# Keeping two kinds of operand sums of the output stage on chip for both pairs, and loading the first residual rows later

## The chip, the cores and the metric

The kernel runs on one core of a Trainium2 chip. The metric is the device time of one execution in microseconds (us); lower is better. The kernel before took 1652.37 us, the median of 3 runs (1649.89 to 1652.61).

## The reference

Two layers over 512 tokens of width 2048. What matters here is the end of each layer: one output projection with a 2048 x 2048 weight, a norm over the 2048 columns, and the residual. All arithmetic is float32.

```python
def hybrid_layer(x, w_in, w_out, g_pre, g_post, ...):
    h = rmsnorm(x, g_pre)
    z = h @ w_in
    ...   # gated linear attention gives o_gla, chunked attention gives o_att
    y = jnp.concatenate([o_gla, o_att], axis=-1) @ w_out
    return x + rmsnorm(y, g_post)

def reference(x, w_in, w_out, g_pre, g_post, ...):
    h = x
    for l in range(DEPTH):
        h = hybrid_layer(h, w_in[l], w_out[l], g_pre[l], g_post[l], ...)
    return h
```

## The kernel before, in words

**Products.** Weights come in blocks of 512 columns. Two blocks make a pair, and a pair is multiplied in Strassen-Winograd form: seven products P1 to P7 instead of eight. Each runs over four chunks c of the contracted dimension. One product for one chunk is 12 matmuls of 128x128 by 128x512 (line 523): every float32 number is split into a high and a low part, and three of the four part products are kept. Below, "a product" means one name for one chunk, such as P6 of chunk 2.

**What a product needs.** On the weight side each job passes four steps: `load` (line 187, a 512 KB DMA on SP's queue), `bring` (line 218, a 512 KB load of the token operand from DRAM into one of the four tiles tagged `sa`, where that operand isn't on chip), `high` (line 238, for most kinds a sum or difference of two weight blocks on DVE at lines 246 or 249, and a copy to the high part on ACT at line 257) and `low` (line 260, the rest, on DVE at line 263, into one of three tiles). `ahead` (line 313) keeps these steps three to five products ahead of the matmuls. On the token side P1, P2 and P4 take plain blocks; P5 takes the sum S1, P6 takes S2, P3 takes S4 and P7 takes S3 (table `LEFT`, line 160).

**The output stage** is `paired_out` (line 1570). Its first pair is columns 0 to 1023 of the output weight (`n` = 0), its second pair the rest (`n` = 2). Chunks go in the order 2, 3, 0, 1 (`C_END`). The order of products is: P1 of the second pair, P1 of the first, P2 of the second, P2 of the first. Then the first pair's P5 (four chunks), the middle (P6 2, P3 2, P6 3, P3 3, P6 0, P6 1, P3 0, P3 1), P7 and P4, and then the same for the second pair: 56 products.

**The sums** of this stage are made by `paired_sums` (line 1432), chunk after chunk, four for each: S1, S2, S4, S3. Each is one DVE addition over 128x512 (line 1447) and a split into high and low parts (a cast on ACT at line 113, a subtraction on DVE at line 114). The result goes into a tile and from there to DRAM through GpSimd's queue (line 1456). S1 has a tile for each chunk (`g6`, `g7`, `g14`, `g15`), and the first pair reads it there; S2, S4 and S3 take turns in two tiles, `g2` and `g3`. `bring` (line 236) loads them back: S2, S4 and S3 for each pair, S1 for the second. A sum's inputs come from DRAM by `load_parts` (line 1423). For chunks 2 and 3 they lie in `sa` tiles (two each), for chunk 0 in `a110` and `a111`, for chunk 1 in two `sa` tiles again. The fourth input is on chip as `og_full`, in a tile of the ring `t2`, which has eight.

**Order.** Side work (attention heads, sums, the finish of tokens) is written as generators, and `pump` (line 323) advances them: `rate` steps after each product. `tc.issue_after` puts one instruction behind another on its engine. The tile framework then orders each engine's instructions by a simulated timeline, with program order as priority, and places the waits. The sums of chunks 0 and 1 begin once the first result of the second pair's P2 is taken (`"first" in issued`). `project` (line 1519) takes a result tile: a square on ACT and a multiplication with the norm's gain on DVE (line 1529). The gains of the stage are loaded by `load_gains` (line 1585) into `a112` and `a113`, and in layer 0 twice more by `load_gain` (line 1513).

**Residual rows.** `load_tokens` (line 620, DMAs at line 616) loads the rows that are added to the result: half 0 into `g6`, `g7`, `g12`, `g13`, half 1 into `g9`, `g10` and four smaller tiles. Before, both halves are issued on GpSimd's queue after the first pair's P7 and P4 of chunk 2, when all sums have been written out. `finish` (line 1556) uses them from the second pair's P7 (layer 0) or P4 (layer 1) on, and in layer 0 goes on with `prep_half` (line 762), which makes the next layer's operands in the tiles `a11..` and `a12..`.

Of the kernel before, what the change touches and what calls it, by code (L numbers as in the profile page):

```python
# [9 lines left out]
F32R = mybir.dt.float32r  # L10
BF16 = mybir.dt.bfloat16
AF = mybir.ActivationFunctionType
ALU = mybir.AluOpType
# [3 lines left out]
P = 128  # L17
# [3 lines left out]
W = 512  # L21
# [14 lines left out]
def hybrid_trunk(  # L36
# [141 lines left out]
    class Job:  # L178
# [39 lines left out]
        def bring(self):  # L218
# [6 lines left out]
            if end and name == "S1" and not p.get("second"):  # L225
                return
# [193 lines left out]
    class Pair:  # L420
# [60 lines left out]
        def operand(self, job, k, c):  # L481
            if job.a is not None:
                return job.a
            if self.end and k == "P5":
                until(lambda: ("S1", c) in A)
                return A["S1", c]
# [400 lines left out]
    def layer(l):  # L887
# [544 lines left out]
        def paired_sums():  # L1432
            spare = 0
            for i, c in enumerate(C_END):
                while c not in og_full or c not in parts and i < 3 or i > 1 and "first" not in issued:
                    yield
                if c not in parts:
                    load_parts(c, [rtile("sa", (2, 512), F32R) for _ in range(2)])
                    yield
                a11, a21, a12, _ = parts[c]  # L1440
                a22 = og_full[c]
                for name, out, in0, in1, op in (
                    ("S1", a22, a21, a22, ALU.subtract), ("S2", a22, a22, a11, ALU.subtract),
                    ("S4", a12, a12, a22, ALU.add), ("S3", a21, a11, a21, ALU.subtract),
                ):
                    with tc.issue_after(last_out[0] or last_state[0]):
                        nc.vector.tensor_tensor(out=out, in0=in0, in1=in1, op=op)
# [5 lines left out]
                    z = slot(tag, [2, 512], F32R)  # L1453
                    with tc.issue_after(last_cast[0]):
                        split(z[:, 0, :], z[:, 1, :], out)
# [43 lines left out]
        values.run(early_rest(C_IN)[-4:], rate=6 if paired else 4, after=fetch_operands)  # L1499
# [252 lines left out]
```

## Time and profile before

| what | value |
|---|---|
| median of the runs | 1652.37 us |
| the profiled execution's own time | 1650.46 us |
| its span on the core | 1648.7 us |
| TensorE (PE) busy | 97% of the span |
| VectorE (DVE) busy | 78% |
| ScalarE (ACT) busy | 57% |
| GpSimd (POOL) busy | 10% |
| mean granted TensorE clock | 0.988 of full speed |
| HBM read, written | 403.50 MB, 65.82 MB |

How to read it: the page gives each engine's busy time; a busy PE is not a PE at its peak, because matmuls are pipelined, so the pace is best taken from start to start of matmuls, or from a stretch's length over its number of products. The waits view says which instruction waited for what, with the total, the count and the longest wait. The windows view gives for a stretch its length, each engine's busy time (and instructions), the granted clock, the busy share of the DMA engines and the GB/s moved. The timeline lists start, length and the idle time before an instruction, with what ended it.

### The profile page before, as it was taken

The numbers are of one execution on the slowest core, as the hardware profiler recorded it, in microseconds if no ns is written. First come the engines' busy times: TensorE is split into PE (matmuls) and PEld (weight loads), VectorE is DVE, ScalarE is ACT, GpSimd is POOL, SyncE is SP. The second block draws the span as 40 slices with busy tenths as digits, with TensorE's granted clock in tenths as the row PEclk, the third lists the DMA queues.
The fourth block names the chain that finished last, engine by engine and source line by source line (L and its number), as shares of the span: only waits on it lengthen the run. The fifth ranks groups of instructions, "written<-read, shape, count | busy, mean of one in ns | idle before, by whom it ended". The sixth has DMA issues, their size and how long they took to land.

```text
span 1648.7 us, 24344 instructions
## 1 busy us (share of the span) xinstructions
PE 1597.6 (97%) x8722; PEld 1344.8 (82%) x8722; DVE 1293.2 (78%) x1600; ACT 946.7 (57%) x1562; POOL 172.9 (10%) x290
## 2 busy tenths in 40 slices
PE   9999999999999999979999999999999999998797
PEld 6787889999988876657877888899999887766575
DVE  6788976877876776958879888868688767869588
ACT  8565544555676545635596555446567765556253
POOL 1131000000001001120132100000010000011101
PEclk9999999999999999989999999999999999999898
DMA  9999966858776696989969898768596857968996
GB/s 373 342 342 351 320 232 233 302 193 295 255 244 222 219 345 242 331 311 387 342 230 349 302 337 320 262 222 289 180 310 213 280 172 273 370 226 301 350 355 229
DMA packets 150553, 472.02 MB, mean 286 GB/s; under 512 B 16428, under 2 KB 35892, under 8 KB 150432
## 3 DMA queue, kind: packets, MB, share of 16 engines
q1 hardware_dynamic: 128384, 394.18, 68.0%
q0 software_dynamic: 21472, 75.33, 11.8%
q8 instruction: 69, 1.13, 0.3%
q10 hardware_dynamic: 576, 0.95, 0.2%
q14 instruction: 52, 0.43, 0.1%
HBM read 403.50 MB, written 65.82 MB: 285 GB/s over the span
## 4 chain that ended last, share of the span: by engine, by line
PE 75%; DMA 10%; DVE 6%; issue 6%; ACT 2%; POOL 1%; SPq 0%; POOLq 0%; ACTq 0%; DVEq 0%
PE mm L523 47%; PE mm L508 20%; DMA raw<-in_w_dram 5%; DVE wl L263 3%; PE ax L1122 2%; DMA H<-in_w_dram 2%; DMA sa<-oS 2%; DMA sa<-A 1%; DVE H L246 1%; PE ax L1328 1%; PE ax L1105 1%; ACT wh L257 1%; PE ax L1292 1%; PE ax L717 1%; PE ax L1085 1%
## 5 line engine op out<-in xcount | busy, mean ns | idle before, releaser
L523 PE MATMUL mm<-wh,sa 128*128 128x512 f32 x1280 | 419.2, 401 | 28.1 <-DMA sa<-oS 22.7
L257 ACT CAST wh<-H 128x1024 fp32r<-128x1024 f32 x263 | 275.9, 1051 | 238.1 <-PE mm L523 99.9
L263 DVE TENSOR_TENSOR wl<-H,wh 128x1024 fp32r<-128x1024 f32 (+1 forms) x265 | 321.7, 1217 | 100.3 <-PE mm L523 41.2
L263 DVE TENSOR_TENSOR wl<-raw,wh 128x1024 fp32r<-128x1024 f32 x240 | 292.8, 1221 | 100.0 <-PE mm L523 46.8
L257 ACT CAST wh<-raw 128x1024 fp32r<-128x1024 f32 x240 | 252.3, 1052 | 195.3 <-PE mm L523 107.2
L523 PEld LDWEIGHTS mm<-wh,sa 128*128 128x128 f32 x1280 | 243.8, 192 | 91.9 <-issue 20.8
L523 PE MATMUL mm<-wh,g 128*128 128x512 f32 x960 | 300.0, 391 | 0.0
L523 PE MATMUL mm<-wh,a 128*128 128x512 f32 x896 | 289.7, 396 | 2.9 <-ACT pc L446 1.6
L246 DVE TENSOR_TENSOR H<-H,raw 128x1024 f32<-128x1024 f32 x192 | 232.7, 1220 | 31.1 <-DMA raw<-in_w_dram 22.3
L523 PE MATMUL mm<-wl,sa 128*128 128x512 f32 x640 | 255.1, 399 | 0.2 <-DVE wl L263 0.2
L508 PE MATMUL mm<-sa,wh 128*128 128x256 f32 x1280 | 236.0, 285 | 0.0
L523 PEld LDWEIGHTS mm<-wh,g 128*128 128x128 f32 x960 | 181.0, 189 | 37.4
L523 PEld LDWEIGHTS mm<-wh,a 128*128 128x128 f32 x896 | 166.7, 188 | 46.8 <-issue 8.4
L508 PEld LDWEIGHTS mm<-sa,wh 128*128 128x128 f32 x1280 | 199.5, 191 | 0.3
L523 PE MATMUL mm<-wl,g 128*128 128x512 f32 x480 | 188.8, 393 | 4.3 <-DVE wl L263 3.9
L508 PE MATMUL mm<-sa,wl 128*128 128x256 f32 x640 | 180.7, 283 | 0.0
L523 PE MATMUL mm<-wl,a 128*128 128x512 f32 x448 | 177.2, 397 | 2.6 <-DVE wl L263 2.6
L523 PEld LDWEIGHTS mm<-wl,sa 128*128 128x128 f32 x640 | 122.9, 192 | 27.2 <-DVE wl L263 1.3
L508 PEld LDWEIGHTS mm<-sa,wl 128*128 128x128 f32 x640 | 122.3, 191 | 0.1
L523 PEld LDWEIGHTS mm<-wl,g 128*128 128x128 f32 x480 | 90.5, 189 | 26.9 <-DVE wl L263 8.2
L523 PEld LDWEIGHTS mm<-wl,a 128*128 128x128 f32 x448 | 84.2, 188 | 24.1 <-DVE wl L263 4.9
L249 DVE TENSOR_TENSOR raw<-H,raw 128x1024 f32<-128x1024 f32 x72 | 87.8, 1219 | 9.0 <-DMA raw<-in_w_dram 9.0
(205 smaller groups left out, 1807.7 us busy)
## 6 DMA issues: line engine op xcount, KB each, us to landing
raw<-in_w_dram SPq DMA_DIRECT2D x360, 512.0 KB, 5.3
sa<-S SPq DMA_DIRECT2D x128, 512.0 KB, 4.7
H<-in_w_dram SPq DMA_DIRECT2D x71, 512.0 KB, 6.2
sa<-oS SPq DMA_DIRECT2D x56, 512.0 KB, 6.9
S<-g POOLq DMA_DIRECT2D x32, 512.0 KB, 6.1
g<-S SPq DMA_DIRECT2D x32, 512.0 KB, 5.2
sa<-A SPq DMA_DIRECT2D x32, 512.0 KB, 5.8
oS<-g POOLq DMA_DIRECT2D x32, 512.0 KB, 5.9
```

The source lines that it names most:

```text
L246: nc.vector.tensor_tensor(out=h, in0=h, in1=r, op=ALU.add)
L249: nc.vector.tensor_tensor(out=r, in0=h, in1=r, op=ALU.subtract)
L257: last_cast[0] = nc.scalar.copy(self.wh, src).ins
L263: last_low[0] = nc.vector.tensor_tensor(out=self.wl[:, kk, :], in0=self.src[:, kk, :], in1=self.wh[:, kk, :].bitcast(F32), op=ALU.subtract ...
L508: nc.tensor.matmul(dst, lhs[:, kk, f], a[:, part, tok], start=(fresh and kk == 0 and m == 0 and ft % 2 == 0), stop=(c == self.last and kk ...
L523: mm = nc.tensor.matmul(out_ps[t], a[:, part, tok], rhs[:, kk, :], start=(fresh and kk == 0 and m == 0), stop=(c == self.last and kk == 1 ...
L717: mm = nc.tensor.matmul(gate_ps[l][g : g + 32, half * 256 : (half + 1) * 256], gate_w[l][:, kh * 8 + c * 2 + kk, :], full[half, c][:, kh, ...
L1085: nc.tensor.matmul(ps[:, :n], self.ql[:, t], self.kh[:, :n], start=False, stop=True)
L1105: nc.tensor.transpose(ps[:, j * P : (j + 1) * P], self.prob[i][:, j * P : (j + 1) * P], ident)
L1122: nc.tensor.matmul(o, self.pt[i][:, j * P : (j + 1) * P], av[hd // 4, j // 2][:, j % 2, (hd % 4) * P : (hd % 4 + 1) * P], start=(j == 0), ...
L1292: mm = nc.tensor.matmul(self.ps_u[cc][:, tt * 256 : (tt + 1) * 256], kd[p][r, tt, hk], self.gv[p][r, tt, hv], start=True, stop=True,).ins
L1328: nc.tensor.matmul(self.ps_o[cc * 64 : (cc + 1) * 64, tt * 256 : (tt + 1) * 256], gqT[h // 2][:, h % 2, n * 64 : (n + 1) * 64], self.st[q] ...
```

## The change

S1 and S3 of the output stage stay in their tiles for both pairs: they are neither written to DRAM nor loaded. S1 takes `g6`, `g7`, `g12`, `g13`; S3 takes `a120` to `a123`, whose earlier content is the operand of P2. S2 and S4 still go through DRAM, now by four tiles. The order of the sums is new: S1, then S2 and S4 for chunks 2 and 3, the same for chunks 0 and 1, then S3 for all four. The inputs of chunk 1 go to `a112` and `a113`. Gains are loaded one at a time into `t2` tiles on GpSimd's queue. The first half of the residual rows is loaded after the second pair's P5. The next layer's preparation waits for the second pair's P7 before it writes `a12..`. Three rates go from 6 to 4.

```diff
@@ Job.bring
-            if end and name == "S1" and not p.get("second"):
+            if end and name in ("S1", "S3"):
                 return
@@ Pair.operand
-            if self.end and k == "P5":
-                until(lambda: ("S1", c) in A)
-                return A["S1", c]
+            if self.end and k in ("P5", "P7"):
+                until(lambda: (LEFT[k], c) in A)
+                return A[LEFT[k], c]
@@ prep_half
-    def prep_half(l, half, xs):
+    def prep_half(l, half, xs, free=lambda: True):
         for ch in (HALF0, HALF1)[half]:
+            while half == 0 and ch >= 4 and not free():
+                yield
             yield from prep_chunk(l, half, ch, xs)
@@ paired_sums
-            spare = 0
-            for i, c in enumerate(C_END):
-                while c not in og_full or c not in parts and i < 3 or i > 1 and "first" not in issued:
+            early, late = C_END[:2], C_END[2:]
+            order = products(early, "S1") + [(n, c) for c in early for n in ("S2", "S4")]
+            order += products(late, "S1") + [(n, c) for c in late for n in ("S2", "S4")] + products(C_END, "S3")
+            through = 0
+            for name, c in order:
+                while c not in og_full or c not in parts or c in late and "first" not in issued:
                     yield
-                if c not in parts:
-                    load_parts(c, [rtile("sa", (2, 512), F32R) for _ in range(2)])
+                while name == "S3" and ("out", "P2", c) not in passed:
                     yield
...
-                    if name == "S1":
-                        tag = ("g6", "g7", "g14", "g15")[i]
-                    else:
-                        tag = ("g2", "g3")[spare % 2]
-                        spare += 1
+                if name == "S1":
+                    tag = {2: "g6", 3: "g7", 0: "g12", 1: "g13"}[c]
+                elif name == "S3":
+                    tag = f"a12{c}"
+                else:
+                    tag = ("g2", "g3", "g14", "g15")[through % 4]
+                    through += 1
...
+                if name in ("S1", "S3"):
+                    A[name, c] = z
+                else:
                     last_put[0] = nc.gpsimd.dma_start(so_d[l][name, c], flat(z)).ins
-                    if name == "S1":
-                        A["S1", c] = z
-                    made.add((l, True, name, c))
-                    yield
+                made.add((l, True, name, c))
+                yield
@@ layer
-        values.run(early_rest(C_IN)[-4:], rate=6 if paired else 4, after=fetch_operands)
+        values.run(early_rest(C_IN)[-4:], rate=4, after=fetch_operands)
@@ load_gain
-        def load_gain(n):
+        def load_gain(n, q=nc.sync):
...
@@ finish
-                yield from prep_half(l + 1, pair, xs)
+                yield from prep_half(l + 1, pair, xs, lambda: not paired or ("end", "P7", C_END[3]) in passed)
@@ paired_out
-            def load_gains(n, tag):
...
             def side(n):
                 def f(k, c):
+                    passed.add(("out", k, c) if n == 0 else ("end", k, c))
                     if n and k == "P1" and c in C_END[:2]:
                         load_parts(c, [rtile("sa", (2, 512), F32R) for _ in range(2)])
                     if (n, k, c) == (0, "P1", C_END[3]):
-                        load_gains(2, "a113")
-                        load_gains(0, "a112")
-                        load_parts(C_END[2], [slot(tag, [2, 512], F32R) for tag in ("a110", "a111")])
-                    if n and not last and (k, c) == ("P3", C_END[3]):
-                        gains[3] = load_gain(3)
-                    if n and not last and (k, c) == ("P7", C_END[3]):
-                        gains[2] = load_gain(2)
-                    if n == 0 and k in ("P7", "P4") and c == C_END[0]:
-                        until(lambda: all((l, True, z, i) in made for z in ("S1", "S2", "S3", "S4") for i in range(4)))
+                        gains[2], gains[0] = load_gain(2, nc.gpsimd), load_gain(0, nc.gpsimd)
+                        for i in range(2):
+                            load_parts(C_END[2 + i], [slot(tag, [2, 512], F32R) for tag in (f"a11{2 * i}", f"a11{2 * i + 1}")])
+                    elif (k, c) == ("P6", C_END[2]):
+                        gains[n + 1] = load_gain(n + 1, nc.gpsimd)
+                    elif (k, c) == ("P4", C_END[0]):
+                        gains[n] = load_gain(n, nc.gpsimd)
+                    if (n, k, c) in ((2, "P5", C_END[3]), (0, "P4", C_END[0])):
+                        i = int(n == 0)
                         with tc.issue_after(last_put[0]):
-                            held["xs", int(k == "P4")] = load_tokens(int(k == "P4"), x_src, nc.gpsimd)
+                            held["xs", i] = load_tokens(i, x_src, nc.gpsimd)
...
-                pairs[i].run(products(C_END, k), rate=6 if k == "P1" else 4, after=side(2 * i))
+                pairs[i].run(products(C_END, k), rate=4, after=side(2 * i))
```

More of the change, by code (lines that the diff above doesn't have):

```diff
@@ L1441, in paired_sums @@
                 a22 = og_full[c]
[L1442 to L1447, printed above, removed]
-                    if name == "S1":
-                        tag = ("g6", "g7", "g14", "g15")[i]
-                    else:
-                        tag = ("g2", "g3")[spare % 2]
-                        spare += 1
-                    z = slot(tag, [2, 512], F32R)
-                    with tc.issue_after(last_cast[0]):
-                        split(z[:, 0, :], z[:, 1, :], out)
+                out, in0, in1, op = {
+                    "S1": (a22, a21, a22, ALU.subtract), "S3": (a21, a11, a21, ALU.subtract),
+                    "S2": (a22, a22, a11, ALU.subtract), "S4": (a12, a12, a22, ALU.add),
+                }[name]
+                with tc.issue_after(last_out[0] or last_state[0]):
+                    nc.vector.tensor_tensor(out=out, in0=in0, in1=in1, op=op)
+                if name == "S1":
[5 more added lines that the diff above has]
+                    through += 1
+                z = slot(tag, [2, 512], F32R)
+                with tc.issue_after(last_cast[0]):
+                    split(z[:, 0, :], z[:, 1, :], out)
+                if name in ("S1", "S3"):
+                    A[name, c] = z
+                else:
                     last_put[0] = nc.gpsimd.dma_start(so_d[l][name, c], flat(z)).ins
-                    if name == "S1":
-                        A["S1", c] = z
-                    made.add((l, True, name, c))
-                    yield
+                made.add((l, True, name, c))
+                yield
         gv = {}
@@ L1511, in layer @@
         YS = (("g8", "g11", "g14", "g15"), ("g0", "g1", "g2", "g3"))
-        def load_gain(n):
+        def load_gain(n, q=nc.sync):
             gp = t2()
             src = g_post[l, n * W : (n + 1) * W]
-            nc.sync.dma_start(gp, bass.AP(tensor=src.tensor, offset=src.offset, ap=[[0, P], [1, W]]))
+            q.dma_start(gp, bass.AP(tensor=src.tensor, offset=src.offset, ap=[[0, P], [1, W]]))
             return gp
@@ L1583, in consume @@
                 return f
-            def load_gains(n, tag):
-                row = slot(tag, [2, W])
-                src = g_post[l, n * W : (n + 2) * W]
-                nc.gpsimd.dma_start(
-                    row.rearrange("p a b -> p (a b)"),
-                    bass.AP(tensor=src.tensor, offset=src.offset, ap=[[0, P], [1, 2 * W]]),
-                )
-                gains[n], gains[n + 1] = row[:, 0, :], row[:, 1, :]
             def side(n):
                 def f(k, c):
+                    passed.add(("out", k, c) if n == 0 else ("end", k, c))
                     if n and k == "P1" and c in C_END[:2]:
@@ L1640, in paired_out @@
                 del A[1, 1, c]
-                del A["S1", c]
+                del A["S1", c], A["S3", c]
             del A["O", 0]
```

## The prediction, made before the changed kernel ran

> **What bounds the kernel now.** I read the page first. It puts PE at 97% of the span, so only time in which PE waits, or runs slowly, can be won. Of its groups, one row carries a large wait.
>
> ```profile
> PE 1597.6 (97%) x8722; PEld 1344.8 (82%) x8722; DVE 1293.2 (78%) x1600; ACT 946.7 (57%) x1562; POOL 172.9 (10%) x290
> ...
> L523 PE MATMUL mm<-wh,sa 128*128 128x512 f32 x1280 | 419.2, 401 | 28.1 <-DMA sa<-oS 22.7
> ```
>
> `sa<-oS` is the load of a sum in the output stage (line 236). To see where this falls I cut both layers' output stages at the borders of the products, which I found by counting line 523's matmuls in twelves. The first block is layer 0: P5, the middle and P7 of the first pair, then P5 and the middle of the second. The other is layer 1, without the last. Columns: length, then busy time of PE, weight loads, DVE, ACT, POOL; granted clock, DMA share, GB/s.
>
> ```profile
> 687.92:704.33 16.41, 13.63 (x50) 10.02 (x49) 16.41 (x21) 9.01 (x15) 2.66 (x5) 0.90 0.82 281
> 704.33:742.51 38.18, 28.43 (x97) 21.51 (x96) 20.96 (x23) 13.17 (x18) 7.96 (x15) 0.82 0.89 330
> 742.51:754.83 12.32, 11.54 (x49) 8.93 (x48) 9.42 (x10) 4.75 (x8) 0.00 (x0) 0.99 1.03 403
> ...
> 765.71:777.64 11.93, 11.53 (x49) 8.83 (x48) 11.56 (x11) 7.57 (x13) 0.00 (x0) 1.00 1.01 395
> 777.64:799.40 21.76, 21.76 (x97) 18.02 (x96) 16.87 (x16) 10.57 (x12) 0.00 (x0) 1.00 0.85 299
> ```
>
> ```profile
> 1501.96:1517.15 15.19, 12.04 (x49) 8.86 (x48) 15.19 (x19) 8.66 (x14) 2.13 (x4) 1.00 0.85 303
> 1517.15:1558.19 41.04, 28.70 (x98) 21.28 (x97) 22.77 (x24) 13.34 (x18) 8.48 (x16) 0.84 0.82 309
> 1558.19:1570.20 12.01, 11.30 (x50) 9.06 (x48) 9.79 (x10) 4.74 (x8) 0.00 (x0) 0.99 1.03 405
> ...
> 1581.08:1592.96 11.88, 11.66 (x49) 8.78 (x48) 11.37 (x11) 7.06 (x12) 0.00 (x0) 1.00 0.99 380
> ```
>
> The second pair's middle is the yardstick: eight products in 21.76 us without a gap, 2.72 us a product, at a full clock. Against it four products should take 10.88 us. So the excess is, for layers 0 and 1: P5 16.41 - 10.88 = 5.53 and 15.19 - 10.88 = 4.31 (9.84); the middle 16.42 and 19.28 (35.70); P7 1.44 and 1.13 (2.57); the second pair's P5 1.05 and 1.00 (2.05). The two P5 stretches differ from the middle in kind: there DVE is busy for the whole length (16.41 of 16.41, 15.19 of 15.19) and is the limit. In the middle it has 20.96 of 38.18, and the limit is something else. The timeline of PE there:
>
> ```profile
> 711.78 0.69 PE L523 MATMUL mm<-wh,sa 128*128 128x512 f32 x1 [1.86 <-DMA sa<-oS]
> 712.27 0.63 PE L523 MATMUL mm<-wl,sa 128*128 128x512 f32 x1
> 712.70 1.05 PE L523 MATMUL mm<-wh,sa 128*128 128x512 f32 x2
> 713.55 0.63 PE L523 MATMUL mm<-wl,sa 128*128 128x512 f32 x1
> ...
> 737.25 0.77 PE L523 MATMUL mm<-wh,sa 128*128 128x512 f32 x1 [5.38 <-DMA sa<-oS]
> ```
>
> After a wait of 1.86 us the three matmuls from 712.27 to 713.55 start 0.43 us apart, where 2.72 / 12 = 0.227 us is normal: each wait is paid once as idle time and again as a slow clock (0.82 in the middle's row).
>
> Why are the loads late? The next rows are from SP's timeline, then DVE's for both layers.
>
> ```profile
> 696.89 0.33 SPq L236 DMA_DIRECT2D sa<-oS  x1
> ...
> 707.24 3.04 SPq L236 DMA_DIRECT2D sa<-oS  x2
> ```
>
> ```profile
> 688.64 2.35 DVE L246 TENSOR_TENSOR H<-H,raw 128x1024 f32<-128x1024 f32 x2
> 690.91 1.22 DVE L263 TENSOR_TENSOR wl<-H,wh 128x1024 fp32r<-128x1024 f32 x1
> ...
> 696.18 0.69 DVE L114 TENSOR_TENSOR g<-sa,g 128x512 fp32r<-128x512 f32 x1
> ...
> 721.28 1.29 DVE L114 TENSOR_TENSOR g<-sa,g 128x512 fp32r<-128x512 f32 x2
> ```
>
> ```profile
> 1536.76 1.28 DVE L114 TENSOR_TENSOR g<-sa,g 128x512 fp32r<-128x512 f32 x2
> ```
>
> The load at 696.89, the second of the stage, goes out just as a split that reads an `sa` tile ends (696.18 + 0.69): it waits for one of the four tiles, which hold the inputs of the sums. The third goes out at 707.24, 0.2 us after P6 of chunk 2 has ended (704.33 + 2.72 = 707.05): it takes that product's tile. The inputs of chunk 1 keep two tiles until the splits at 721.28, so until then only two are left to the loads, and one load costs more than a product:
>
> ```profile
> sa<-oS SPq DMA_DIRECT2D x56, 512.0 KB, 6.9
> ```
>
> ```profile
> oS<-g POOLq DMA_DIRECT2D x32, 512.0 KB, 5.9
> ```
>
> And the splits are late because S2, S4 and S3 share two tiles, each busy until its write has landed (5.9 us): the waits view has ACT's cast held by just that.
>
> ```profile
> ACT g L113 <- DMA oS<-g: 13.4, 10, 3.9
> ```
>
> **The change part by part.** *Traffic.* Per layer S1 (second pair) and S3 (both) lose 12 loads, S1 and S3 lose 8 writes, and 8 writes instead of 12 use four tiles instead of two, each tile twice. *The ring.* Chunk 1's inputs leave the `sa` ring. Chunks 2 and 3 keep two of its tiles until their S4 is split and two until their S3 is, which now comes last. *Middle.* With four tiles and sums that are written early, a load can be issued three products ahead, 8.2 us for 6.9 us, as in the second pair's middle, which ran without a gap. I take 2 us a layer as left over, for S3's hold on the ring: 35.70 - 4.0 = 31.7 us gained. Ends: 0 left, or the first two waits stay (first rival). *P7.* Its operands are on chip: 2.57 to 0.5 a layer, 1.6 gained. *Second pair's P5.* Four loads less in a stretch whose DMA share is 1.01; half of the excess goes, 1.0 gained.
>
> *The first pair's P5* gets worse. The sums are no longer spread out by two tiles, so they press into the stretch where DVE is the limit. From the start of P2 (four products before 687.92, so 677.0) to the last P5 `low`, DVE must do four additions and six `low`s of 1.13 us each in a row (two end after 2.35 us at 688.64, one takes 1.22 alone, so 2.35 - 1.22), 11.3 us; four multiplications of line 1529 and one split of a head's output at 0.60 (likewise 1.29 - 0.69), 3.0; and ten sums at two operations each, 12.0. Together 26.3 us, then one product: 677.0 + 26.3 + 2.72 = 706.1, where P5 ended at 704.33: 1.8 us lost. In layer 1 it is 1501.96 - 10.88 + 29.0 = 1520.1 against 1517.15: 2.9 lost. The short waits there can bring the slow clock: layer 0's row has 0.90, layer 1's 1.00. I add 1.0 a layer. In all 6.7 us lost. Ends: if DVE takes P5's work first, nothing is lost and the 9.8 us of excess may go; if late head work joins, the second rival.
>
> The row at 711.78 shows the slow pace after 1.86 us of idling. The Trainium skill, page "TensorE: Matmul & The Clock Gate", Part 1, says that the clock halves after an idle window of about 3.4 us; by that rule P5's short waits would cost no clock and the sum would be 2 us lower, 1623. The trace disagrees about the length.
>
> *Residual rows.* Four loads of half 0 now wait on GpSimd's queue for the second pair's P5, which reads S1 in their tiles. Behind them on POOL stand the gains of the second pair and the small operations of `finish`, none due before P3's end, 21.8 us later.
>
> ```profile
> DMA to landing us min/median/max: 6.9/15.4/19.8
> ```
>
> That is line 616's time from issue to landing. 19.8 us at worst is just inside the eight products to P7, where DVE needs them in layer 0 (P4, 10.9 us later, in layer 1). Cover: the second pair's middle; without it DVE would stand at line 1550 with the `low`s behind it, some 2 us. I take 0. *Gains.* In `t2` tiles they can be late for the multiplication of P2's result, with P5's additions behind it on DVE:
>
> ```profile
> DMA to landing us min/median/max: 4.0/4.2/4.6
> ```
>
> That is line 1588's landing; 0 to 4.2 us a layer, I take 0, since they are issued a whole P2 (four products, 10.9 us) ahead. *Rates and `prep_half`.* In the P1 and P2 stretch ahead PE has no idle time, so fewer side steps there leave its length alone:
>
> ```profile
> 630.00:677.02 47.02, 47.02 (x217) 32.54 (x217) 32.85 (x50) 26.63 (x53) 7.13 (x10) 1.00 0.65 228
> ```
>
> The wait in `prep_half` binds nobody: `finish` takes about ten steps before chunk 4, at 1.5 a product nearly seven products from P7 on, and P7 has four.
>
> *Sum.* 31.7 + 1.6 + 1.0 - 6.7 = 27.6 us. The profiled execution took 1650.46 us (span 1648.7 and 1.8 around it), so 1622.9 there; the median is 1.9 higher: 1652.4 - 27.6 = 1624.8, about 1625. With the ends above (4 us less left over, P5 unharmed and half of its excess gone, 4.9) about 1609; with gains late and a little more left in the middle about 1636. Own range 1611 to 1634.
>
> **The rivals.** *The ring stays half full.* If S3 of chunks 2 and 3 is split only after P5, the third and fourth loads again wait for products. Then the excess of these four products stays, 19.09 - 10.88 = 8.2 and 21.91 - 10.88 = 11.0 us, instead of the 4:
>
> ```profile
> 707.04:726.13 19.09, 14.72 (x49) 10.71 (x48) 11.25 (x13) 6.48 (x9) 5.23 (x10) 0.82 0.85 283
> 1519.88:1541.79 21.91, 14.87 (x50) 10.53 (x48) 13.04 (x16) 8.21 (x11) 5.30 (x11) 0.84 0.74 260
> ```
>
> 15.2 us dearer, 1640. For it: S3 is last in the new order. Against: the ten sums fit before P5's end by the sum above.
>
> *DVE takes it back.* With 4 steps instead of 6 the last heads come later, and their states and gates move from the P1 stretch (DVE 32.85 of 47.02) into P2 and P5. Lines 1314 and 1346 there:
>
> ```profile
> 630.00:677.02 47.02, 5.74 (x12) 1.00 0.65 228
> ```
>
> ```profile
> 630.00:677.02 47.02, 3.48 (x8) 1.00 0.65 228
> ```
>
> 0.48 x 4 + 0.44 x 2 = 2.8 us a unit; two units and 1.6 of slow clock are 7.2 a layer: 1639. Against: PE's work there, which feeds them, isn't moved.
>
> *Slower: the loads wait for the last S3.* If P6's first load gets the tile that S3's inputs hold, and that split comes as late as the last pair did before (721.28 + 1.29 = 722.6, 1536.76 + 1.28 = 1538.0), it lands 6.9 us later. Then 12 products (32.6 us) follow, and P7 ends at 762.1 against 754.83, and at 1577.6 against 1570.20: 7.3 and 7.4 lost instead of gained, 1652.4 + 14.7 - 1.0 = 1666. It turns slower when the split ends after 754.8 - 32.6 - 6.9 = 715.3. For it: SP works in order, so weight loads stand behind such a wait. Against: the load at 707.24 took the first tile to come free, not the next in turn.
>
> *Nothing saved.* The sums come no earlier, because the side steps, not the two tiles, hold them: 1651. Against: the tile wait of 13.4 us above, and 16 steps in the first pair's P2 for ten sums.
>
> **How the numbers follow.** My forecast 0.70; ring half full 0.10; DVE 0.08; slower 0.08; nothing saved 0.04. Faster is 0.70 + 0.10 + 0.08 = 0.88. About 0.2% is what a measurement here can tell from no change. The range, 1610 to 1642, takes in the first three cases but for their edges and leaves out the last two.
>
> **What would show it.** Right: `sa<-oS` 32 instead of 56, `oS<-g` 16 instead of 32, HBM read about 391 MB; the first pair's middle near 24 us at a clock of 1.00; P5 near 18 us with DVE full. The ring would show as a third load issued only when P6 of chunk 2 ends. Wrong altogether: the middle still over 30 us, or a new wait of DVE for gains or residual rows.

## The result, and the profile after

The kernel after took 1636.88 us (median of 4 runs, 1636.54 to 1639.25), the kernel before 1651.54 us beside it (4 runs, 1649.89 to 1652.61): a ratio of 0.9915, with a 95% interval of 0.9898 to 0.9932. That is 14.7 us faster and half of the 27.6 us forecast: inside the whole range (1610 to 1642), which takes in three cases, but slower than the forecast's own range (1611 to 1634). The profiled execution took 1636.54 us, its span 1634.8, which is 13.9 us less than before.

The page of after, its engines, its group of the output stage, and the loads:

```profile
PE 1589.1 (97%) x8722; PEld 1340.2 (82%) x8722; DVE 1292.8 (79%) x1600; ACT 948.3 (58%) x1562; POOL 160.2 (10%) x282
...
L523 PE MATMUL mm<-wh,sa 128*128 128x512 f32 x1088 | 350.5, 395 | 8.6 <-ACT mm L453 3.8
...
sa<-oS SPq DMA_DIRECT2D x32, 512.0 KB, 5.7
```

The loads are 32, as the diff says, and the wait for them, 22.7 us before, no longer stands in the group's row. What PE waits for instead is in the waits view (total, count, longest), first before, then after:

```profile
PE mm L523 <- DMA sa<-oS: 22.7, 10, 5.4
...
PE mm L523 <- DVE wl L263: 6.7, 12, 1.3
```

```profile
PE mm L523 <- DVE wl L263: 14.7, 16, 2.5
...
PE ax L731 <- DVE g L741: 5.3, 1, 5.3
...
PE mm L523 <- DMA sa<-oS: 3.6, 3, 2.1
```

The wait for DMA fell by 19 us, and waits for DVE rose by 13: 8 for the low part of the weights, 5 for one copy at the border of the two layers. The windows of after, for each layer the first pair's P5, its middle and P7, then the second pair's P5 (columns as in the prediction):

```profile
686.76:702.03 15.27, 11.93 (x49) 8.85 (x48) 15.27 (x20) 9.82 (x16) 0.31 (x1) 1.00 0.61 225
702.03:729.46 27.43, 23.66 (x98) 17.70 (x96) 19.70 (x20) 10.30 (x13) 5.06 (x10) 1.00 0.89 326
729.46:740.34 10.88, 10.88 (x50) 9.01 (x48) 9.64 (x11) 5.87 (x8) 0.54 (x1) 1.00 0.69 218
...
751.22:764.78 13.56, 11.58 (x50) 8.78 (x48) 13.07 (x14) 7.69 (x12) 1.59 (x3) 1.00 1.02 411
...
1493.69:1510.37 16.68, 12.23 (x49) 8.77 (x48) 16.68 (x21) 10.87 (x19) 0.08 (x1) 1.00 0.64 238
1510.37:1538.83 28.46, 24.51 (x97) 18.86 (x96) 19.76 (x20) 10.23 (x13) 5.29 (x10) 0.94 0.86 317
1538.83:1550.79 11.96, 11.36 (x50) 8.75 (x48) 9.27 (x11) 5.96 (x10) 0.54 (x1) 1.00 0.48 134
...
1562.79:1578.06 15.27, 12.76 (x49) 10.08 (x48) 14.55 (x14) 7.66 (x13) 1.60 (x3) 0.89 0.90 357
```

Against the windows of before, both layers together:

| stretch | before | after | change | forecast |
|---|---|---|---|---|
| first pair's P5 | 31.60 | 31.95 | +0.35 | +6.7 |
| middle | 79.22 | 55.89 | -23.3 | -31.7 |
| P7 | 24.33 | 22.84 | -1.5 | -1.6 |
| second pair's P5 | 23.81 | 28.83 | +5.0 | -1.0 |
| from layer 0's last matmul to layer 1's first | 1.0 | 10.2 | +9.2 | 0 |

The remaining parts are small: P4 in layer 1 +1.1, the second pair's P7 and P4 in layer 0 -1.6, the first 14 products of layer 1 -3.3 (0.9 of it in the first product, where PE in before also ran eight of the preparation's transposes, which in after lie ahead of it; the rest was not traced). The sum is -14.0, the spans' difference 13.9.

The border of the two layers is a new place of loss. In after's timeline of PE, line 731 makes the transposes with which the next layer's operands begin; the second fence is ACT's timeline there (line 594 squares the new rows for the next norm, line 745 copies what was transposed).

```profile
808.80 1.47 PE L731 MATMUL ax<-cst,g 128*128 128x128 f32 x12
815.60 3.39 PE L731 MATMUL ax<-cst,g 128*128 128x128 f32 x16 [5.33 <-DVE g L741]
```

```profile
812.49 1.05 ACT L594 ACTIVATE t<-g 128x1024 bf16<-128x1024 f32 x1
...
813.53 1.05 ACT L594 ACTIVATE t<-g 128x1024 bf16<-128x1024 f32 x1
...
814.57 1.56 ACT L745 ACTIVATE g<-ax,gcol 128x256 f32<-128x256 f32 x4
```

The twelve transposes run only after the last product (808.80). The copies come 4.3 us after them, behind squares which in before ran two microseconds after layer 1's first product (826.3 and 824.1 us), and PE idles 5.33 us. The 16 transposes behind that wait run at a slow clock: from 808.96 to 818.75 us the granted clock was 0.83. In before the same twelve ran among the products, 6.5 us ahead of the last one's end, and the copy followed at once (PE's line, then ACT's):

```profile
816.89 1.47 PE L731 MATMUL ax<-cst,g 128*128 128x128 f32 x12
...
817.86 1.57 ACT L745 ACTIVATE g<-ax,gcol 128x256 f32<-128x256 f32 x4
```

### The profile page after: what moved, and what is told of

The parts are those of the page before. It is cut to its first block, busy times and chain, and to the rows that moved or that the text cites. A ratio compares the mean times of both kernels' runs of the same rounds, so it can differ in the third digit from the quotient of the medians.

```text
span 1634.8 us, 24266 instructions
## 1 busy us (share of the span) xinstructions
PE 1589.1 (97%) x8722; PEld 1340.2 (82%) x8722; DVE 1292.8 (79%) x1600; ACT 948.3 (58%) x1562; POOL 160.2 (10%) x282
## 3 DMA queue, kind: packets, MB, share of 16 engines
HBM read 391.44 MB, written 57.43 MB: 275 GB/s over the span
## 4 chain that ended last, share of the span: by engine, by line
PE 78%; DMA 7%; issue 6%; DVE 6%; ACT 1%; POOL 1%; SPq 0%; POOLq 0%; DVEq 0%; ACTq 0%
PE mm L523 48%; PE mm L508 20%; DMA raw<-in_w_dram 3%; DVE wl L263 2%; PE ax L1124 2%; DMA H<-in_w_dram 2%; PE ax L1330 1%; DVE H L246 1%; PE ax L1107 1%; DMA sa<-oS 1%; PE ax L1294 1%; DMA sa<-A 1%; PE ax L1087 1%; PE ax L1086 1%; PE ax L1085 1%
## 5 line engine op out<-in xcount | busy, mean ns | idle before, releaser
L523 PE MATMUL mm<-wh,sa 128*128 128x512 f32 x1088 | 350.5, 395 | 8.6 <-ACT mm L453 3.8
L523 PE MATMUL mm<-wh,a 128*128 128x512 f32 x1024 | 331.7, 396 | 2.7 <-ACT a L113 1.3
L523 PE MATMUL mm<-wh,g 128*128 128x512 f32 x1024 | 319.8, 391 | 0.2 <-ACT mm L547 0.2
L523 PEld LDWEIGHTS mm<-wh,sa 128*128 128x128 f32 x1088 | 203.7, 189 | 58.4 <-ACT mm L453 5.3
L523 PEld LDWEIGHTS mm<-wh,a 128*128 128x128 f32 x1024 | 191.5, 188 | 52.9 <-issue 9.3
L523 PEld LDWEIGHTS mm<-wh,g 128*128 128x128 f32 x1024 | 193.0, 188 | 40.6 <-ACT mm L547 0.9
L523 PE MATMUL mm<-wl,sa 128*128 128x512 f32 x544 | 214.1, 394 | 3.2 <-DVE wl L263 3.2
L523 PE MATMUL mm<-wl,g 128*128 128x512 f32 x512 | 202.2, 395 | 9.9 <-DVE wl L263 9.7
L523 PE MATMUL mm<-wl,a 128*128 128x512 f32 x512 | 201.4, 394 | 1.8 <-DVE wl L263 1.8
L523 PEld LDWEIGHTS mm<-wl,g 128*128 128x128 f32 x512 | 96.5, 188 | 36.6 <-DVE wl L263 16.9
L523 PEld LDWEIGHTS mm<-wl,sa 128*128 128x128 f32 x544 | 102.5, 188 | 26.2 <-DVE wl L263 4.6
L523 PEld LDWEIGHTS mm<-wl,a 128*128 128x128 f32 x512 | 96.2, 188 | 24.4 <-DVE wl L263 4.0
L249 DVE TENSOR_TENSOR raw<-H,raw 128x1024 f32<-128x1024 f32 x72 | 87.8, 1219 | 11.1 <-DMA raw<-in_w_dram 10.9
```

The source lines that it names most:

```text
L249: nc.vector.tensor_tensor(out=r, in0=h, in1=r, op=ALU.subtract)
L523: mm = nc.tensor.matmul(out_ps[t], a[:, part, tok], rhs[:, kk, :], start=(fresh and kk == 0 and m == 0), stop=(c == self.last and kk == 1 ...
```

## The experiments

Each run is timed beside the kernel before on the same chip. The columns: P5 with the middle, the stretch from the first pair's P7 to the end of the second pair's P5 (12 products, 32.6 us at full pace), each for layers 0 / 1, and the gap at the border, from layer 0's last matmul to layer 1's first.

| run | us | ratio to before (95%) | P5 + middle | P7 to 2nd P5 | gap |
|---|---|---|---|---|---|
| before | 1650.1 to 1651.5 | | 54.6 / 56.2 | 35.1 / 34.8 | 1.0 |
| after | 1636.9 | 0.9915 (0.9898 to 0.9932) | 42.7 / 45.1 | 35.3 / 39.2 | 10.2 |
| ring_only | 1643.5 | 0.9959 (0.9943 to 0.9975) | 47.9 / 50.6 | 39.9 / 38.8 | 1.1 |
| tiles_only | 1639.6 | 0.9937 (0.9921 to 0.9954) | 48.5 / 48.7 | 38.8 / 36.1 | 1.1 |
| ring_tiles | 1642.7 | 0.9953 (0.9939 to 0.9966) | 48.3 / 46.8 | 38.5 / 42.0 | 1.6 |
| rows_late | 1650.4 | 0.9998 (0.9988 to 1.0007) | 55.3 / 56.6 | 35.3 / 34.8 | 1.0 |
| gain_sp | 1634.2 | 0.9903 (0.9888 to 0.9918) | 41.6 / 43.7 | 36.3 / 39.0 | 9.6 |
| no_hold | 1633.9 | 0.9907 (0.9888 to 0.9927) | 42.6 / 43.4 | 36.0 / 39.8 | 10.6 |
| rates6 | 1640.0 | 0.9938 (0.9922 to 0.9955) | 46.2 / 47.8 | 35.0 / 34.6 | 9.4 |
| s3_last | 1629.6 | 0.9870 (0.9855 to 0.9884) | 40.5 / 42.2 | 35.8 / 37.2 | 10.6 |
| border_order | 1630.8 | 0.9876 (0.9857 to 0.9895) | 42.5 / 43.7 | 36.6 / 39.7 | 4.4 |
| mult_pool | 1625.5 | 0.9846 (0.9831 to 0.9861) | 41.9 / 43.3 | 35.3 / 35.4 | 1.0 |
| mult_out | 1619.3 | 0.9810 (0.9794 to 0.9826) | 42.1 / 41.7 | 33.5 / 33.9 | 1.9 |
| combo | 1621.6 | 0.9815 (0.9800 to 0.9830) | 40.4 / 43.3 | 35.9 / 35.3 | 1.0 |

**Which part of the change wins the middle.** `ring_only` and `tiles_only` each take one small part of it alone, on top of the kernel before.

```diff
-                    load_parts(c, [rtile("sa", (2, 512), F32R) for _ in range(2)])
+                    load_parts(c, [slot(tag, [2, 512], F32R) for tag in ("g12", "g13")])
```

> The kernel before with one edit: the inputs of the sums of chunk 1 lie in g12 and g13 and not in two of the four sa tiles. Theory R (the ring of four tiles is what delays the loads): the first pair's middle loses most of its excess over 21.76 us (16.4 and 19.3 us), at least the waits at P6 of chunks 3 and 0, about 19 us with their slow pace; 1632 to 1637. Theory T (late sums through two tiles are what delays them): the middle stays over 34 us in both layers, 1648 to 1652.

```diff
-                        tag = ("g2", "g3")[spare % 2]
+                        tag = ("g2", "g3", "g12", "g13")[spare % 4]
```

> The kernel before with one edit: S2, S4 and S3 take turns in four tiles (g2, g3, g12, g13) and not in two. Theory T: the sums come earlier, the middle falls to under 30 us in both layers, 1630 to 1637. Theory R: the ring is still half full until the last sums of chunk 1, but these come earlier, so only the last wait (5.4 us at P3 of chunk 1) shrinks; 1642 to 1648.

Both help, neither alone is enough. The middle is 34.5 and 36.2 us with the ring freed, 32.4 and 32.3 with four tiles, against 38.2 and 41.0 before and 27.4 and 28.5 after. `ring_tiles` has both, with the gains in `t2` tiles as in after, so that chunk 1's inputs can lie in `a112` and `a113`:

```diff
-                    load_parts(c, [rtile("sa", (2, 512), F32R) for _ in range(2)])
+                    load_parts(c, [slot(tag, [2, 512], F32R) for tag in ("a112", "a113")])
...
-                        tag = ("g2", "g3")[spare % 2]
+                        tag = ("g2", "g3", "g12", "g13")[spare % 4]
```

> The kernel before with the two small parts of the change together: chunk 1's inputs outside the sa ring, and four tiles instead of two for S2, S4 and S3 (with the gains in t2 tiles, which frees the room); S1 and S3 still pass through DRAM in the old order of the sums. Theory M, what the middle lacked was tiles: these two take most of its excess, the middle falls to 27 to 30 us a layer and the time to 1632 to 1638. Rival, residency is what counts (12 loads less a layer): the middle stays at 31 to 34 and P7 at 13 or more, since its loads still come, 1638 to 1643.

The time agrees with the rival, the middle nearly with theory M: 30.5 and 28.1 us. But of the 20.6 us won there over both layers, P7, which still loads S3, takes back 6.9, and P5 4.8 (36.4 against 31.6). P7's rows:

```profile
734.53:749.32 14.79, 11.82 (x49) 9.14 (x48) 10.97 (x12) 5.06 (x8) 0.54 (x1) 0.97 1.03 406
...
1544.99:1561.44 16.45, 12.99 (x49) 9.48 (x48) 10.85 (x12) 5.16 (x8) 0.55 (x1) 0.90 1.03 407
```

There the DMA share is 1.03, as it was in before's shorter P7, and PE's long waits (2.15 us in layer 0, 1.95 and 1.23 in layer 1) are for `sa<-oS`. In after, P7 loads no sum and has 10.88 and 11.96 us at a share of 0.69 and 0.48. So the tiles alone move part of the wait from the middle to P7, where only leaving out the loads removes it.

**The residual rows alone.** `rows_late` is before with only that move in the program.

```diff
-                    if n == 0 and k in ("P7", "P4") and c == C_END[0]:
-                        until(lambda: all((l, True, z, i) in made for z in ("S1", "S2", "S3", "S4") for i in range(4)))
+                    if (n, k, c) in ((2, "P5", C_END[3]), (0, "P4", C_END[0])):
```

> The kernel before with only the residual rows of half 0 loaded behind the second pair's P5 instead of the first pair's P7. The prediction's zero: the gap between the layers stays at 1.0 us, the second pair's P5 at 11.9, 1649 to 1653. Rival, the rows make the second P5 longer (13.6 and 15.3 in after, with them in flight): 13 us or more, 1652 to 1656; and if they land late for the finish, the gap grows by 3 or more.

No change, and a second P5 of 11.8 and 11.7 us. But the loads did not move there. GpSimd's queue was far ahead, and in before's layout their tiles come free early: half 0 left at 726.84 to 734.67 us in layer 0, in the first pair's middle, where it also leaves in before (from 723.38 on). In after S1 holds the tiles, and half 0 leaves in the second P5. The first line is from `rows_late`, the second from after:

```profile
726.84 0.53 POOL L616 DMA_DIRECT2D g<-in_x_dram  x1
...
754.50 0.53 POOL L616 DMA_DIRECT2D g<-in_x_dram  x1 [8.59 <-PE mm L523]
```

So this run does not test what the rows cost. After's trace says something of it: PE's longest waits in the second P5 end at 756.19 and 1565.92 us, and the first row of each layer leaves at 754.50 and 1570.36, too late to have caused them. No addition of line 1557 waits for a row either.

**Three causes of the border that were not.** `gain_sp` loads the second pair's last gain on SP's queue instead of GpSimd's; `no_hold` takes the new wait out of `prep_half`.

```diff
-                        gains[n] = load_gain(n, nc.gpsimd)
+                        gains[n] = load_gain(n, nc.sync if n else nc.gpsimd)
```

> The changed kernel with one edit: the second pair's gain for its last two results is loaded on SP's queue again, not on GpSimd's. Theory A (this load, issued at 807.06 behind the writes of finished tokens and landed at 813.03, holds DVE in order, and DVE holds the transposes at the border of the layers): the wait of 5.3 us and the slow pace after it go, the step of 9.2 us at the border falls to under 2, and the time is about 1628 to 1630. Theory B (the new wait of the next layer's preparation for the second pair's P7 bunches the transposes): nothing changes, 1637, and the wait of the transposes on DVE stays.

```diff
-                yield from prep_half(l + 1, pair, xs, lambda: not paired or ("end", "P7", C_END[3]) in passed)
+                yield from prep_half(l + 1, pair, xs, lambda: True)
```

> The changed kernel with one edit: the next layer's preparation does not wait for the second pair's P7 in program order (the tile framework still keeps S3's tiles until they have been read). Theory A: nothing changes, 1637. Theory B: the step of 9.2 us at the border of the layers goes, about 1628.

The gap stays at 9.6 and 10.6, and neither time can be told from after's: neither the gain nor the hold. `rates6` puts the rates back.

```diff
-        values.run(early_rest(C_IN)[-4:], rate=4, after=fetch_operands)
+        values.run(early_rest(C_IN)[-4:], rate=6 if paired else 4, after=fetch_operands)
...
-                pairs[i].run(products(C_END, k), rate=4, after=side(2 * i))
+                pairs[i].run(products(C_END, k), rate=6 if k == "P1" else 4, after=side(2 * i))
```

> The kernel after with the rates of side steps back at 6 (the last four products of the values' pair, and P1 of the output stage). The prediction's zero for the rates: the same within 2 us, 1633 to 1637, and P5 and the middle as in after (15.3 and 27.4, 16.7 and 28.5). Rival, head work that comes late at the lower rate sits on DVE in front of the sums: S2 and S4 of chunks 0 and 1 come earlier, P5 and the middle together are 3 us or more a layer shorter, 1628 to 1631.

Neither held: P5 and the middle are 3.5 and 2.7 us longer, the stretch behind them shorter by 0.3 and 4.6 (as it would be if DVE works ahead while PE waits), and the gap is 9.4 us. The median is 3.1 us above after's, with intervals that overlap; the trace is that of the fastest of the four. The lower rates do no harm.

**The order at the border.** `border_order` changes only where instructions stand.

```diff
+                    mm = nc.tensor.transpose(
...
+                    if half == 0 and ch < 4:
+                        last_turned[0] = mm
...
+                last_prep[0] = nc.scalar.activation(d, ps[:, kk * 256 : (kk + 1) * 256], AF.Copy, scale=g).ins
...
+                with tc.issue_after(last_turned[0]) if self.end and (k, c) == ("P4", C_END[3]) and last_turned[0] and self.l == 0 else nullcontext():
+                    self.matmuls(job, k, c)
...
+            with tc.issue_after(last_prep[0]) if l and half == 0 else nullcontext():
+                square_sum(ss[:, j : j + 1], xs[j])
```

> The kernel after with only the order of instructions at the border of the layers changed: ACT's four row squares of half 0 (line 594) go behind ACT's last copy of that half, and the first twelve transposes of the next layer go ahead of the last P4 product. Theory O, the order alone costs the time: in after the transposes' input was ready at 804.8 us but they ran at 808.8, and ACT ran two squares (2.1 us) and three others before the first copy at 814.6. Then the gap between the layers falls from 10.2 to 3 to 5 us, and the time by 3 to 6 us, to 1629 to 1633. Theory D, DVE is late with the finish of the tokens whatever the order: DVE ends its work ahead of the copies at 812 to 814, so the gap stays at 8 or more, and the time at 1634 to 1637.

Theory O holds. PE's timeline of this kernel:

```profile
805.98 1.47 PE L734 MATMUL ax<-cst,g 128*128 128x128 f32 x12
...
810.49 1.97 PE L734 MATMUL ax<-cst,g 128*128 128x128 f32 x16 [0.26 <-DVE g L746]
814.28 0.50 PE L523 MATMUL mm<-wh,a 128*128 128x512 f32 x1 [1.82 <-ACT a L113]
```

The transposes stand one product earlier, the idle time before the second group falls from 5.33 to 0.26 us, its 16 transposes take 1.97 us instead of 3.39 (the clock is 1.00 there), the gap falls to 4.4, the time to 1630.8. The P4 stretch ahead is 1.4 us longer, since it now holds the transposes, so the net is 4.4 us: about half of the border's loss was the order that the tile framework chose, on PE and ACT together. What lies behind the choice remained open, and so did the rest.

**DVE.** `mult_pool` moves half of the gain multiplications to POOL.

```diff
-            last_out[0] = nc.vector.tensor_tensor(
+            mult = (nc.gpsimd if pool else nc.vector).tensor_tensor(
...
-                    project(2 * h + t, n + j, settled(src, comb), gains[n + j])
+                    project(2 * h + t, n + j, settled(src, comb), gains[n + j], pool=comb is not None)
```

What goes to POOL is also no longer the instruction behind which the sums are put on DVE (`last_out`).

> The kernel after with 8 of the 16 gain multiplications a layer, those whose source lies in SBUF (0.68 us each on DVE), on POOL instead of DVE. Theory D, DVE is the limit from the first pair's P7 to the border of the layers: DVE loses 4 x 0.6 = 2.4 us of its 33.4 in the 35.3 us up to the end of the second pair's P5, which PE waited 2.0 us for, and three more before the finish of token 1. Then the second pair's P5 falls from 13.6 and 15.3 to 11 to 12.5 us, the gap between the layers from 10.2 to under 5, and the time by 6 to 11 us, to 1626 to 1631. Rival, the loads of the residual rows (DMA share 1.02 there) or the clock make the second P5 long: it stays at 13 to 15 us, and the gap at 8 to 10, since the finish then waits for POOL; 1634 to 1638.

The gap (1.0) and the second P5 (12.2 in both layers) came as theory D said, and the time (1625.5) just below its range, but not by its mechanism. In layer 0 the whole stretch from P7 on took 35.3 us as in after, what P5 won being lost in P4 (12.3 instead of 10.9). In layer 1 it fell from 39.2 to 35.4 us with DVE as busy as before (34.47 us; 34.38 in after), so not all of after's loss there is a matter of how much DVE has to do. The groups of line 1536 and the instructions of line 246 (ns: minimum, median, maximum) show why:

```profile
L1536 POOL TENSOR_TENSOR g<-t,t 128x512 f32<-128x512 f32 x16 | 36.4, 2279 | 112.2 <-DVE t L461 91.1 <-DVE t L463 17.5 <-DVE sm L1551 3.5
...
L246 DVE TENSOR_TENSOR H<-H,raw x192: 1204/1222/2330, 73.8 to 1595.6; 128x1024 f32<-128x1024 f32 x192
```

POOL takes 2.28 us for what DVE did in 0.68, and a DVE instruction beside it up to 2.33 us, where the longest of line 246 in after was 1.26. DVE gained nothing: 16 multiplications left it, and its busy time over the whole run rose from 1292.8 to 1299.1 us. What the run did gain at the border is again the order: with the multiplications off DVE the framework put the twelve transposes at 802.54, 6.6 us ahead of the last product's end.

`mult_out` tests DVE's part without POOL: the same eight multiplications are left out, and the addition ahead of each writes the result straight into its place (`result_row`), which also saves a tile of `t2` each; no run separates the two.

```diff
-                    project(2 * h + t, n + j, settled(src, comb), gains[n + j])
+                    if comb is None:
+                        project(2 * h + t, n + j, src, gains[n + j])
+                    else:
+                        row = result_row(2 * h + t, n + j)
+                        comb(row)
+                        project(2 * h + t, n + j, row, None)
```

> The kernel after without the 8 gain multiplications a layer that mult_pool gave to POOL: they are left out, so half of the results enter the norm's last step without their gain. In mult_pool the DVE instruction beside each of POOL's multiplications (2.2 us) took 2.31 us instead of 1.22, so DVE saved nothing there, and from the first pair's P7 to the end of the second pair's P5 it took 35.3 us a layer, as in after's layer 0 (35.3). Theory D, DVE's work bounds that stretch: without 4 x 0.6 us it takes 32.6 to 34 us in both layers; the gap between the layers is 1 to 3 us, and the time 1615 to 1621. Rival, the stretch is bound by something else (the weights' loads, the clock) and mult_pool's gain was the order of the instructions at the border alone: the stretch stays at 35 or more, the time at 1623 to 1627.

Theory D holds with its numbers. The windows of the stretch in both layers, for before, after, mult_pool and mult_out:

```profile
742.51:777.64 35.13, 33.94 (x145) 26.77 (x144) 30.95 (x31) 18.03 (x29) 0.00 (x0) 1.00 1.02 402
1558.19:1592.96 34.77, 33.84 (x145) 26.84 (x144) 30.85 (x31) 18.16 (x29) 0.00 (x0) 1.00 1.01 397
```

```profile
729.46:764.78 35.32, 33.34 (x146) 26.80 (x144) 33.41 (x35) 19.50 (x30) 2.67 (x5) 1.00 0.91 327
1538.83:1578.06 39.23, 35.86 (x145) 27.86 (x144) 34.38 (x35) 19.59 (x30) 2.68 (x5) 0.96 0.81 293
```

```profile
727.27:762.61 35.34, 33.52 (x146) 26.82 (x144) 35.03 (x30) 19.75 (x30) 11.62 (x9) 1.00 0.86 311
1527.62:1562.99 35.37, 33.81 (x146) 26.73 (x144) 34.47 (x30) 19.77 (x30) 11.57 (x9) 1.00 0.85 302
```

```profile
727.40:760.86 33.46, 33.06 (x146) 26.87 (x144) 31.04 (x30) 19.35 (x30) 1.60 (x3) 1.00 0.93 347
1526.64:1560.56 33.92, 33.01 (x146) 26.95 (x144) 31.58 (x32) 19.96 (x30) 1.60 (x3) 1.00 0.89 340
```

The third number in brackets counts DVE's instructions. For the same twelve products DVE ran 31 in before and 35 in after. In before it had done the others ahead, while PE waited for loads. In after there is less of such time: DVE enters the stretch four instructions behind. Take 4 x 0.6 us of work from it, and the stretch is 1.9 us shorter in layer 0 and 5.3 in layer 1, where a wait of 2.52 us had also brought the slow clock (0.89 in the second P5's row).

DVE's amount of work is not the whole of it. On the way to PE's longest wait in each layer's second P5, DVE itself waited for a weight block, 0.49 us in layer 0 (at 752.04) and 1.25 in layer 1:

```profile
1563.51 1.22 DVE L246 TENSOR_TENSOR H<-H,raw 128x1024 f32<-128x1024 f32 x1 [1.25 <-DMA H<-in_w_dram]
```

The `low` that PE waited for until 1565.92 us came right behind it. In `mult_out` DVE stood idle for 1.12 and 0.76 us a few microseconds ahead of that P5, and PE did not wait in it. What such a late load costs by itself was not tested.

**S3 behind S2.** The sums of chunks 0 and 1 were late in after although S3 is last in program order. `s3_last` holds S3 back.

```diff
-                while name == "S3" and ("out", "P2", c) not in passed:
+                while name == "S3" and ("out", "P5", c) not in passed:
```

> The kernel after with S3's four sums held back in program order until P5 of their chunk, so that on DVE they fall behind S2 of chunks 0 and 1. Theory S, the middle's 12.4 us of excess come from S2 and S4 of chunks 0 and 1, which DVE reached 10 to 20 us after S1 because S3's eight operations (4.8 us) and the weights' stood ahead: their writes go out 2 to 4 us sooner, the middle falls from 27.4 and 28.5 to about 25 each, 1630 to 1633. Rival, the ring: the tiles that hold S3's inputs come free later, the third and fourth load of the stage wait, and the middle stays at 27 to 30: 1635 to 1640.

It is 7.3 us faster than after, but the middle gave little of it (26.4 and 28.0 us), so theory S has the time but not the place. P5 gave most, 14.1 and 14.2 instead of 15.3 and 16.7. The additions on DVE's timeline, in after (where `sa<-sa` and `a<-a` are S3, `t<-t,a` is S2):

```profile
680.96 1.29 DVE L1451 TENSOR_TENSOR sa<-sa 128x512 f32<-128x512 f32 x2
...
684.43 0.68 DVE L1451 TENSOR_TENSOR a<-a 128x512 f32<-128x512 f32 x1
...
691.38 0.68 DVE L1451 TENSOR_TENSOR t<-t,a 128x512 f32<-128x512 f32 x1
```

and in s3_last, followed by SP's loads there:

```profile
688.50 0.69 DVE L1451 TENSOR_TENSOR t<-t,a 128x512 f32<-128x512 f32 x1
...
691.37 0.69 DVE L1451 TENSOR_TENSOR t<-t,a 128x512 f32<-128x512 f32 x1
...
694.31 1.29 DVE L1451 TENSOR_TENSOR sa<-sa 128x512 f32<-128x512 f32 x2
```

```profile
684.38 0.42 SPq L236 DMA_DIRECT2D sa<-oS  x1
...
705.23 0.33 SPq L236 DMA_DIRECT2D sa<-oS  x1
```

The rival's mechanism is there too: the third load went out at 689.22 in after, here at 705.23, when tiles of the ring come free. It costs less than DVE's time in P5 is worth.

**Both together.** `combo` has s3_last's edit and mult_pool's, except for the last layer's second pair.

```diff
+                    project(2 * h + t, n + j, settled(src, comb), gains[n + j], pool=comb is not None and not (last and n))
```

> The kernel after with two earlier edits together: the gain multiplications with a source in SBUF on POOL (except those of the last layer's second pair, where the end waits for them) and S3's sums behind S2 of chunks 0 and 1. If DVE is the limit in both places, the gains add: mult_pool's 11.4 us, s3_last's 7.3 less what both take from the same stretch (the second pair's P5, 2 to 3), and 2 us at the end of the last layer: 1619 to 1624. Rival, S3's gain was DVE time in P5 that POOL's share now frees anyway: no better than 1625.

It takes 1621.62 us, 0.9815 of before (0.9800 to 0.9830), and computes all that before does: the fastest such version here.

## Why the prediction was right, and where it was not

The kernel got faster by the mechanism that was forecast, in the middle and P7, but two losses that the sum did not have took about half of it. The time lies between the forecast (1625) and the rivals at 1639 and 1640; it is inside the whole range because that was drawn over the rivals too.

*Traffic, P7, residual rows, `prep_half`'s wait, rates.* Right: 32 loads, HBM read of 391.44 MB, and 1.5 us from P7, though nearly all of it came in layer 0 (1.4), where the forecast had 0.9 and 0.6. `no_hold` shows a zero where the prediction had one, and putting the rates back gains nothing. The rows' zero fits after's trace, but `rows_late` does not test it. *Gains:* the wait that the prediction named as a sign against it is there, DVE stood 3.3 us in two waits for a gain. `gain_sp` has no such wait, and its time can't be told from after's, so the zero holds within that.

*Middle and first P5.* Their sum was nearly right, their shares were not: two errors of opposite sign, 8.4 and 6.4 us, cancel. Forecast -31.7 + 6.7 = -25.0, measured -23.3 + 0.35 = -23.0. The left-over was taken as 4 us and is (27.43 - 21.76) + (28.46 - 21.76) = 12.4; the loss in P5 was taken as 6.7 and is 0.35. The two share DVE's queue: in `gain_sp`, which differs from after in one load, P5 took 17.2 and 18.1 us and the middle 24.4 and 25.6, with a clock of 0.90 in P5, nearer to the forecast's shares at about the same sum. What DVE does not do in P5 makes S2 and S4 of chunks 0 and 1 late for the middle; in layer 0 their writes landed at 710.32, 714.33 and 716.85 us and their loads left at 710.43, 714.38 and 716.91, so they did not wait for a tile. So the reason given for the left-over, S3's hold on the ring, was wrong in after; that hold came up only in `s3_last`.

*Second pair's P5.* Wrong in sign: forecast -1.0, measured +5.0. The failing step is "Four loads less in a stretch whose DMA share is 1.01; half of the excess goes". First, the stretch did not move less. The prediction itself says further on that four loads of residual rows wait for this P5; they are of 512 KB each like the sums, and three of the four leave in it, the fourth within 1 us behind. By length and rate the stretch moved 5.6 and 5.5 MB, where it had moved 4.7 and 4.5, at a share of 1.02 and 0.90. Second, a high share was not what made PE wait: it waited for DVE's low parts, and `mult_out`, with the rows in it as well, ran that P5 in 10.98 and 10.88 us at a share of 1.02 and 1.01. What part the late weight blocks have stays open.

*The border of the layers.* The prediction had no term for it, and the gap grew by 9.2 us; about 2 of them are transposes that before ran among the products on both sides, which became shorter by as much. The failing step is the sum's silence about everything behind the second pair's P5, whose work the change leaves as it was. Of `finish` it asked whether the residual rows arrive in time ("none due before P3's end"), not whether DVE gets to it in time once PE no longer waits. The rival "DVE takes it back" had the right engine and size (7.2 us a layer, 14.4 in all, against 5.0 + 9.2 measured), but the wrong work: not late heads, but the weights' steps and the finish. `mult_out` shows that the second P5 hangs on DVE's 4 x 0.6 us (with the reserve on `t2` above), and `border_order` that the order which the framework chose is worth about half of the border; the other half, and why its simulated timeline puts the transposes behind the last product in after, stay open.

## What to carry to other kernels

When a wait of the main engine goes, ask which helper used that time to work ahead: add up the helper's work for the next stretches and set it against their full-pace length, since 33 us of work in 33 us of products leaves nothing to catch up with. When loads leave a stretch, ask also which others move into it, and take a load that was moved in the program as moved only when the trace shows it. A high DMA share in a stretch does not say that DMA bounds it; look at what the main engine's few waits there name. And where a framework orders instructions by a simulated timeline, compare the order at every border after a change, also far behind it.

## What the runs showed of the hardware

*The clock.* Waits of about 2 us can bring the slow pace, as in before, but not all of them do. From PE's timeline of after, two waits and the matmuls behind them:

```profile
756.19 0.50 PE L523 MATMUL mm<-wl,g 128*128 128x512 f32 x1 [1.54 <-DVE wl L263]
756.53 0.39 PE L523 MATMUL mm<-wh,g 128*128 128x512 f32 x1
756.76 0.39 PE L523 MATMUL mm<-wl,g 128*128 128x512 f32 x1
...
1565.92 0.67 PE L523 MATMUL mm<-wl,g 128*128 128x512 f32 x1 [2.52 <-DVE wl L263]
1566.39 0.63 PE L523 MATMUL mm<-wh,g 128*128 128x512 f32 x1
1566.82 0.63 PE L523 MATMUL mm<-wl,g 128*128 128x512 f32 x1
```

After 1.54 us the pace is 0.23, after 2.52 it is 0.43; in `border_order` the wait of 1.82 us at 814.28 was followed by 0.23, and in `tiles_only` even one of 3.50 at 1524.04. So the slow clock of 1.0 us a layer that the prediction booked in P5 was not paid in after (1.00 in both rows), but was in `gain_sp` (0.90, 0.91).

The traces also show what sets them apart. The granted clock falls to 0.50 for 3.41 us or a multiple of it, on a fixed grid: in before at 698.27, 711.93 and 722.17 us, four and three times 3.41 apart. What PE did in the 3.41 us ahead seems to decide. Two such pairs of stretches, from before (the wait of 1.86 us) and from after (the one of 1.54):

```profile
708.49:711.90 3.41, 1.55 (x8) 0.97 (x7) 3.34 (x4) 1.04 (x1) 0.97 (x2) 1.00 0.94 376
711.90:715.32 3.42, 3.42 (x9) 2.66 (x10) 0.69 (x1) 0.62 (x1) 0.53 (x1) 0.50 0.93 264
```

```profile
753.68:757.09 3.41, 1.87 (x9) 1.23 (x8) 3.41 (x4) 0.73 (x1) 0.53 (x1) 1.00 1.02 419
757.09:760.50 3.41, 2.96 (x14) 2.12 (x13) 3.41 (x5) 3.14 (x5) 0.53 (x1) 1.00 1.04 414
```

PE was busy for 1.55 us of the first and got 0.50 next; busy for 1.87 it kept 1.00. Ahead of the slow stretch at 1566.09 it was busy for 0.90 us, and the wait of 3.50 us is split by the grid, with 1.55 and 1.77 us busy on its two sides, and brought none. So the limit lies near half of a stretch, but 1.55 us went both ways, and how sharp it is was not measured. The Trainium skill, page "TensorE: Matmul & The Clock Gate", Part 1, has the clock halve after an idle window of about 3.4 us that runs freely and isn't tied to the kernel. The trace agrees on the window and on its running freely, and disagrees in that a window idle for about half could be enough.

*POOL beside DVE.* A multiplication on POOL can cost DVE more time (2.33 instead of 1.22 us for the instruction beside it, 1.1) than it takes off it (0.68). The Trainium skill, page "GPSIMD Engine Reference", section 8, says that GpSimd shares its SBUF interfaces with DVE, with contention when a DVE instruction has two SBUF inputs, as those of line 246 have; the trace agrees. Section 3.1 gives 1.96 times DVE's time for an addition of two inputs; here it was 2.28 against 0.68 us, 3.4 times.
